# Gate units between the first dense units, one power for all key norms, keys a group ahead, and the last head's squares by one-column products

## The chip, the cores and the metric

The kernel runs on one core of a Trainium2 chip. The metric is the device time of one execution in microseconds (us). The core has five engines that the text calls PE (TensorE, the matmuls; PEld is its weight load), DVE (VectorE), ACT (ScalarE), POOL (GpSimd) and SP (SyncE, which here only issues transfers). Each engine takes its instructions in a fixed order, and they meet at semaphores.

## The reference

Two layers over a sequence of 512 tokens, 1024 channels, all in float32. Cut to what matters:

```python
h = rmsnorm(x, pre_mix_g)
proj = h @ w_in                  # q k v z beta decay | SWA q k v | gate A, gate B
y_a = deltanet_branch(...) @ w_up_dn      # 8 heads of 128
y_b = swa_sink_branch(...) @ w_up_sw      # 16 query heads of 64, 2 key heads, window 128
mix = (sigmoid(gate_a) * y_a + sigmoid(gate_b) * y_b) @ w_o
x = x + rmsnorm(mix, post_mix_g)
x = x + rmsnorm(square(relu(rmsnorm(x, pre_mlp_g) @ w_ff1)) @ w_ff2, post_mlp_g)
```

In the DeltaNet branch the keys are scaled to length one (`k * rsqrt(sum(k*k) + EPS)`), a triangular system per chunk and head is solved, a state runs over the chunks, and each head's output is normed: `rmsnorm(o, norm_g) * silu(z)`. The mean of squares of that norm is the "squares" of the title, one number per token and head.

## The kernel before

Activations lie channel by token, `128 x 512` tiles, eight of them for 1024 channels. Every float32 product is made of three passes: each operand is split in a high part (`_h`, rounded) and a low part (`_l`, the rest), and PE runs high by high, low by high and high by low. One **unit** (`mm_a`) makes 128 output channels for all 512 tokens: 8 blocks of 128 input channels x 3 passes = 24 matmuls of 512 columns. A split is one ACT copy (line 419 for weights, 545 for the rest) and one DVE subtraction (420, 546). Weights come in 512 KB chunks over SP, in the fixed order of `chunk_order`, four units ahead (`LOOK`).

A layer goes through these stages; the numbers are the spans in layer 0 of the profile shown below.

- Key, gate and attention stage (about 77 to 234 us). A loop over 16 attention groups `(t, g, e)`: four token tiles `t`, two key heads `g`, two halves `e`. `MIX` says which units ride with each group: `K` a key unit of the DeltaNet branch (`k_unit`), `G` a unit of gate B, `A` one of gate A. Three gate A units are made here (`NA = 3`).
  - `k_unit(h)` makes the keys of a head, their products with themselves in PSUM (`ps_a`, line 909, a ring of one bank called `PK`), takes the diagonal for the squared length (914), adds EPS (916), raises it to the power 0.5 on POOL (918, `irk`), and scales the products by the decay (926) into the triangular matrix `uu`.
  - `att_group` takes the scores (`ps_s`, 1055), a softmax with ACT and DVE, turns the probabilities (`ps_pt`, a bank of the `PS` ring of three), masks them on POOL (`pc`, 1095) and multiplies by the values (`ps_o`, 1102, also `PS`). `att_prep(t)` readies the keys `kT` and values of a token tile; it is called at the start of the tile's first group, after that group's unit in program order.
- First dense units, upward product and solve (about 223 to 299 us). `d_dense(0)` makes value, query and output gate units of head 0 (`ps_vp`, `ps_qp`, `ps_zp`), which use the `PM` ring of two banks; a bank of `vp` or `qp` is held until the causal convolution on DVE (883) has read it. Then eight units of the attention's upward product (`ps_us`) run, with the steps of the triangular solve on DVE between them, and then two gate A units (`NA` to `NA2`, `ps_ga`), stored to DRAM (`gad`).
- Heads (about 299 to 490 us). For each head, `d_inverse` finishes the inverse by small products (`ps_i`), `d_chain` runs the recurrence, and `d_dense(h + 1)` gives PE wide matmuls in between. `d_keys` loads the keys back (`kk`, ring `T[3]`) and `by_token` turns them through DRAM (1236, 1239, 1241). After head 7, three more gate A units run.
- The norm of each head is `d_tail(h)`, a generator whose steps are called by `d_step`: split the squares `w`, sum over channels with a product by ones (`ps_w`), copy one row out, store it to DRAM (`sd`), load it turned (`ff`, so that 512 numbers lie in 128 x 4), take the power -0.5 on POOL (1303), store (`fd`), broadcast to all partitions (`fb`, 1307), and multiply into `y1` (1309).
- Upward product of the DeltaNet branch (`ps_ud`, 490 to 535 us): `yT`, the split of each head's `y1` (line 546), then eight units, the first four of which take heads 0 to 5 before heads 6 and 7. Then output projection, and the MLP.

The order on each engine is not the program order. A planner lays it out ahead of time, from modelled durations: of what it reckons ready it issues, in the main, what stands earliest in the program. Buffers are rings of named tags (`T[0]` to `T[8]`, four each). `tc.keep_in_program_order(i)` keeps an instruction from being put ahead of earlier instructions of its engine.

Of the kernel before, what the change touches and what calls it, by code (L numbers as in the profile page):

```python
# [10 lines left out]
F32 = mybir.dt.float32  # L11
# [9 lines left out]
P = 128  # L21
# [39 lines left out]
def chunk_order(depth):  # L61


    out = []
    for l in range(depth):
        a_in = lambda w, c: out.append(("chunk", w, l, 0, c, 0))
        b_in = lambda w, r, c, n: out.append(("chunk", w, l, r, c, n))
        for a, b in BK:
            out.append(("chunk", "w_bkv", l, a * P, 0, (b - a) * NB))
        for u in range(NQU):  # L70
            a_in("w_q", u * 8)
        n_ = {"K": 0, "G": 0, "A": 0}
        for c in "".join(MIX):
            a_in("w_in", {"K": OFF_K, "G": OFF_GB, "A": OFF_GA}[c] + n_[c] * P)
            n_[c] += 1
        for h in range(H):
            for o in (OFF_V, OFF_Q, OFF_Z):
                a_in("w_in", o + h * P)
            if h == 0:
                for m in range(KT):  # L80
                    a_in("w_up_sw", m * P)
                for m in range(NA, NA2):
                    a_in("w_in", OFF_GA + m * P)
        for m in range(NA2, KT):
            a_in("w_in", OFF_GA + m * P)
        for m in range(KT):
            a_in("w_up_dn", m * P)
        for n in range(2):
            for j in range(4):
                b_in("w_o", j * 256, n * 512, 512)  # L90
        for s in range(4):
            out.append(("up", l, s))
            if s < 3:
                out.append(("seven", "w_ff2", l, s * 1024))
                continue
            for n in range(2):
                for j in range(4):
                    b_in("w_ff2", s * 1024 + j * 256, n * 512, 512)
    return out
# [44 lines left out]
def hybrid_trunk(ctx, tc, x, positions, pre_mix_g, dn_conv_w, dn_a_log, dn_dt_bias, dn_norm_g,  # L144
# [25 lines left out]
    def s1(name, n):  # L170
        return sm.tile([P, n], F32, name=name, bufs=1)
# [14 lines left out]
    def PK(name):  # L186
        return pp.tile([P, 512], F32, name=name, tag="pk", bufs=1)
# [27 lines left out]
    def c4(ap):  # L215
        return ap.rearrange("p (c i) -> p c i", c=4)
# [15 lines left out]
    nc.gpsimd.memset(ban, 0.0)  # L232
    nc.gpsimd.affine_select(out=ban, in_=ban, pattern=[[-1, P]], compare_op=ALU.is_ge, fill=NEG,
                            base=0, channel_multiplier=1)
    pw = const.tile([P, 8], F32, name="pw")
    nc.gpsimd.memset(pw[:, 0:4], -0.5)
    nc.gpsimd.memset(pw[:, 4:8], 0.5)
    mhalf, phalf = pw[:, 0:4], pw[:, 4:8]

    T64 = const.tile([64, 256], F32, name="T64")  # L240
    nc.gpsimd.memset(T64, 0.0)
# [298 lines left out]
    def split(src, hi, lo, sign=1.0):  # L540
        if sign < 0:
            act(out=hi, in_=src, func=AF.Copy, scale=-1.0)
            stt(out=lo, in0=src, scalar=-1.0, in1=hi.bitcast(F32), op0=ALU.mult, op1=ALU.subtract)
            return
        nc.scalar.copy(hi, src)
        tt(out=lo, in0=src, in1=hi.bitcast(F32), op=ALU.subtract)  # L546

    def pair(U, name):
        return U(name + "_h", F32R), U(name + "_l", F32R)
# [100 lines left out]
    for l in range(depth):  # L650
# [238 lines left out]


        cj, irk = [], []

        def k_unit(h):
            if h < 4:
                d = T[5]("D")
                dma(d, dd[h])
            else:
                d = decay_load(h)
            ps = PM("ps_kp")
            mm_a(ps, hT)  # L900
            k_ = conv_silu(ps, 8 + h, T[4], "kk")
            dma(kkd[h], k_)
            if h >= 4:
                decay_of(h, d)
            yield
            ps = PK("ps_a")
            for c in range(NC):
                sl = slice(c * P, (c + 1) * P)
                mm(ps[:, sl], lhsT=k_[:, sl], rhs=k_[:, sl], start=True, stop=True)
            u_ = T[5]("uu")  # L910
            sk_ = sm.tile([P, NC], F32, name="ssk")
            for c in range(NC):
                sl = slice(c * P, (c + 1) * P)
                stt(out=u_[:, sl], in0=ps[:, sl], scalar=1.0, in1=ident, op0=ALU.mult,
                    op1=ALU.mult, accum_out=sk_[:, c:c + 1])
            ts(out=sk_, in0=sk_, scalar1=EPS, scalar2=None, op0=ALU.add)
            ir = sm.tile([P, NC], F32, name="irk", bufs=H + 1)
            ptt(out=ir, in0=sk_, in1=phalf, op=ALU.pow)
            irk.append(ir)
            cc = sm.tile([P, NC], F32, name="cj", bufs=H + 1)  # L920
            nc.vector.reciprocal(cc, sk_)
            tt(out=cc, in0=cc, in1=hc(beta)[:, h, :], op=ALU.mult)
            cj.append(cc)
            for c in range(NC):
                sl = slice(c * P, (c + 1) * P)
                stt(out=u_[:, sl], in0=ps[:, sl], scalar=cc[:, c:c + 1], in1=d[:, sl],
                    op0=ALU.mult, op1=ALU.mult)
            dma(umat(h), c4(u_))
# [20 lines left out]
        def ga_early(m):  # L949
            ga_unit(m, T[5])  # L950
            dma(gad[m], sga[m])
# [82 lines left out]

        def att_group(t, g, e):

            if g == 0 and e == 0:
                if t == 0:
                    att_rope(0)
                att_prep(t)  # L1040
            if (g, e) == (1, 0) and t < NT - 1:
                att_rope(t + 1)
            w0 = max(t - 1, 0) * P
# [33 lines left out]
            for j in range(4):  # L1077
                js = slice(j * P, (j + 1) * P)
                act(out=M[:, js], in_=M[:, js], func=AF.Copy, scale=den[:, j:j + 1])
            yield  # L1080
            ps = PS("ps_pt")
            together = Order(nc.tensor)
# [34 lines left out]
        def steps(n):  # L1117
            for _ in range(n):
                next(sol, None)
# [30 lines left out]
        for u in klate:  # L1150
            fin(u)


        dn = {}

# [134 lines left out]
        def d_tail(h):  # L1290

            w, y1 = dn.pop(("t", h))
            wh, wl = pair(T[5], "w")
            split(w, wh, wl)
            ps = PS("ps_w")
            mm(ps, lhsT=ones_r, rhs=wh, start=True, stop=False)
            mm(ps, lhsT=ones_r, rhs=wl, start=False, stop=True)
            nc.scalar.copy(w[0:1], ps[0:1])
            dma(sd[h:h + 1, :], w[0:1])
            yield  # L1300
            ff = sm.tile([P, NC], F32, name="ff")
            dma(ff, sd[h, :].rearrange("(p j) -> p j", p=P))
            ptt(out=ff, in0=ff, in1=mhalf, op=ALU.pow)
            pdma(fd[h, :].rearrange("(p j) -> p j", p=P), ff)
            yield
            fb = T[6]("fb")
            dma(fb, fd[h, :].partition_broadcast(P))
            yield
            tc.keep_in_program_order(tt(out=y1, in0=y1, in1=fb, op=ALU.mult))

        tails = [d_tail(h) for h in range(H)]

# [64 lines left out]
        for t in range(NT):  # L1377
            tsl = slice(t * P, (t + 1) * P)
            for g in range(2):
                for j in range(g * 4, g * 4 + 4):  # L1380
                    hi, lo = oT[j]
                    split(qt[t][:, j * P:(j + 1) * P], hi[:, tsl], lo[:, tsl])
        turn0 = d_dense(0, lambda: steps(2))
        for m in range(KT):
            ps = PM("ps_us")
            mm_a(ps, oT)
# [3 lines left out]
            steps(2 if m < 6 else 40)  # L1390
            if m == 1:
                turn0()
        for m in range(NA, NA2):
            ga_early(m)

        Pcv, Tcv = inv

        d_load(0, 1, 2, 3)
# [385 lines left out]
```

## Time and profile before

| | |
|---|---|
| median of 3 runs | 1817.6 us (1817.01 to 1820.55) |
| the profiled execution's own time | 1817.76 us |
| its span, first to last instruction | 1816.1 us |
| busy: PE, DVE, ACT, POOL | 1787.7, 1376.8, 998.8, 200.3 us |
| mean granted TensorE clock | 0.998 |

Wide matmuls are pipelined: the profile shows each as 0.39 us long, and one starts every 0.227 us. So a PE that is shown busy can still lose time where two starts lie further apart, and such gaps are read from the starts.

### The profile page before, as it was taken

The numbers are of one execution on the slowest core, as the hardware profiler recorded it, in microseconds if no ns is written. First come the engines' busy times: TensorE is split into PE (matmuls) and PEld (weight loads), VectorE is DVE, ScalarE is ACT, GpSimd is POOL, SyncE is SP. The second block draws the span as 40 slices with busy tenths as digits, with TensorE's granted clock in tenths as the row PEclk, the third lists the DMA queues.
The fourth block names the chain that finished last, engine by engine and source line by source line (L and its number), as shares of the span: only waits on it lengthen the run. The fifth ranks groups of instructions, "written<-read, shape, count | busy, mean of one in ns | idle before, by whom it ended". The sixth has DMA issues, their size and how long they took to land.

```text
span 1816.1 us, 28412 instructions
## 1 busy us (share of the span) xinstructions
PE 1787.7 (98%) x10220; PEld 1511.2 (83%) x10220; DVE 1376.8 (76%) x2576; ACT 998.8 (55%) x2039; POOL 200.3 (11%) x346
## 2 busy tenths in 40 slices
PE   9999999999999999999999999999999999999998
PEld 7887878887788888989888877888877888889896
DVE  6489796888666878888565897878884669698973
ACT  7578732444434656566555887234443347566572
POOL 2013202221101000000020131022111010000000
PEclk9999999999999999999999999999999999999999
DMA  6845447555453255554557453575554533555551
GB/s 221 276 142 184 117 139 232 169 163 152 128 190 135 82 163 153 173 179 147 185 182 239 156 169 105 170 231 162 159 139 148 167 116 104 175 164 161 174 178 55
DMA packets 167071, 294.33 MB, mean 162 GB/s; under 512 B 34497, under 2 KB 83969, under 8 KB 166930
## 3 DMA queue, kind: packets, MB, share of 16 engines
q1 hardware_dynamic: 166418, 292.48, 51.9%
q8 instruction: 80, 1.31, 0.3%
q14 instruction: 61, 0.50, 0.1%
q0 software_dynamic: 512, 0.03, 0.0%
HBM read 246.19 MB, written 46.27 MB: 161 GB/s over the span
## 4 chain that ended last, share of the span: by engine, by line
PE 80%; DVE 8%; ACT 6%; DMA 3%; issue 2%; POOL 1%; SPq 0%; DVEq 0%; POOLq 0%; ACTq 0%
PE ps_f L435 2%; PE ps_f L436 2%; PE ps_f L437 2%; PE ps_zp L435 2%; PE ps_zp L436 2%; PE ps_b L506 2%; PE ps_us L436 2%; PE ps_b L504 2%; PE ps_b L508 2%; PE ps_us L437 2%; PE ps_us L435 2%; PE ps_zp L437 2%; PE ps_ud L436 1%; PE ps_qp L435 1%; PE ps_qp L436 1%
## 5 line engine op out<-in xcount | busy, mean ns | idle before, releaser
L419 ACT CAST wh<-wr 128x1024 fp32r<-128x1024 f32 (+2 forms) x366 | 372.7, 1023 | 416.1 <-PE ps_us L436 62.7
L420 DVE TENSOR_TENSOR wl<-wr,wh 128x1024 fp32r<-128x1024 f32 (+2 forms) x366 | 435.4, 1196 | 170.3 <-ACT wh L419 164.4
L571 POOL TENSOR_TENSOR pr<-pq,pw 128x1 f32<-128x1 f32 x16 | 9.8, 615 | 787.6 <-DVE pq L570 787.6
L435 PE MATMUL ps_f<-g_h,wh 128*128 128x512 f32 x160 | 62.4, 390 | 0.0
L436 PE MATMUL ps_f<-g_l,wh 128*128 128x512 f32 x160 | 62.4, 390 | 0.0
L437 PE MATMUL ps_f<-g_h,wl 128*128 128x512 f32 x160 | 62.2, 389 | 0.0
L1073 ACT ACTIVATE M<-M,nm 128x128 f32<-128x128 f32 x128 | 49.8, 390 | 10.9 <-DVE nm L1068 10.8
L436 PE MATMUL ps_ud<-yT_l,wh 128*128 128x512 f32 x128 | 50.7, 396 | 2.9 <-DVE yT_l L546 2.9
L435 PE MATMUL ps_zp<-h_h,wh 128*128 128x512 f32 x128 | 50.5, 394 | 2.8 <-DVE vv L883 2.8
L436 PE MATMUL ps_qp<-h_l,wh 128*128 128x512 f32 x128 | 53.2, 415 | 0.0
L437 PE MATMUL ps_qp<-h_h,wl 128*128 128x512 f32 x128 | 53.1, 415 | 0.0
L435 PE MATMUL ps_vp<-h_h,wh 128*128 128x512 f32 x128 | 52.8, 413 | 0.0
L437 PE MATMUL ps_vp<-h_h,wl 128*128 128x512 f32 x128 | 52.6, 411 | 0.0
L435 PE MATMUL ps_qp<-h_h,wh 128*128 128x512 f32 x128 | 52.5, 410 | 0.0
L435 PE MATMUL ps_ga<-h_h,wh 128*128 128x512 f32 x128 | 51.4, 402 | 1.0 <-ACT sga L946 1.0
L378 DVE TENSOR_TENSOR wr<-wr 128x512 f32<-128x512 f32 x72 | 47.5, 685 | 6.0 <-DMA wr<-in_weights_dram 5.5
L435 PE MATMUL ps_kp<-h_h,wh 128*128 128x512 f32 x128 | 51.5, 403 | 0.0
L436 PE MATMUL ps_vp<-h_l,wh 128*128 128x512 f32 x128 | 51.2, 400 | 0.0
L435 PE MATMUL ps_gb<-h_h,wh 128*128 128x512 f32 x128 | 51.2, 400 | 0.0
L437 PE MATMUL ps_ga<-h_h,wl 128*128 128x512 f32 x128 | 50.5, 395 | 0.0
L437 PE MATMUL ps_ud<-yT_h,wl 128*128 128x512 f32 x128 | 50.5, 395 | 0.0
L436 PE MATMUL ps_ga<-h_l,wh 128*128 128x512 f32 x128 | 50.5, 394 | 0.0
(449 smaller groups left out, 5958.3 us busy)
## 6 DMA issues: line engine op xcount, KB each, us to landing
wr<-in_weights_dram SPq DMA_DIRECT2D x336, 512.0 KB, 3.7
qT<-qd SPq DMA_DIRECT2D x32, 256.0 KB, 3.5
D<-dd SPq DMA_DIRECT2D x24, 256.0 KB, 2.8
xd<-xo SPq DMA_DIRECT2D x12, 512.0 KB, 2.6
xt<-xd SPq DMA_DIRECT2D x24, 256.0 KB, 6.1
qd<-qf_h SPq DMA_DIRECT2D x16, 256.0 KB, 4.2
qd<-qf_l SPq DMA_DIRECT2D x16, 256.0 KB, 3.4
D<-gd SPq DMA_DIRECT2D x16, 256.0 KB, 4.2
```

Source lines behind the costliest of these rows:

```text
L378: tt(out=o_, in0=i0, in1=i1, op=ALU.add)
L419: nc.scalar.copy(wh[:, :w], wr[:, :w])
L420: sub(out=wl[:, :w], in0=wr[:, :w], in1=wh[:, :w].bitcast(F32), op=ALU.subtract)
L435: mm(ps, lhsT=wh[:, k, :], rhs=hi, start=k == 0, stop=False)
L436: mm(ps, lhsT=wh[:, k, :], rhs=lo, start=False, stop=False)
L437: mm(ps, lhsT=wl[:, k, :], rhs=hi, start=False, stop=k == KT - 1)
L504: mm(pss[t], lhsT=hi[:, tsl], rhs=wh[:, r, :], start=k == 0 and not onto, stop=False, skip_group_check=onto)
L506: mm(pss[t], lhsT=hi[:, tsl], rhs=wl[:, r, :], start=False, stop=False, skip_group_check=onto)
L508: mm(pss[t], lhsT=lo[:, tsl], rhs=wh[:, r, :], start=False, stop=k == KT - 1, skip_group_check=onto)
L571: ptt(out=r, in0=q1, in1=mhalf[:, 0:1], op=ALU.pow)
L1073: act(out=M[:, j * P:(j + 1) * P], in_=M[:, j * P:(j + 1) * P], func=AF.Exp, bias=nm[:, j:j + 1], accum_out=den[:, j:j + 1])
```

## The change

- **Gate units.** The two gate A units `NA` to `NA2` no longer follow the eight `ps_us` units. One is made after the value unit of `d_dense(0)` and one after its query unit, through the call `after()`. Their weight chunks move in `chunk_order` to match.
- **One power.** `k_unit` writes the squared lengths of all heads in one tile `ssk` of 128 x 32. The eight powers of 128 x 4 on POOL become one of 128 x 32 after the attention loop.
- **Bank of the key products.** `ps_a` of odd heads takes a bank of `PS` instead of `PK`.
- **Keys ahead.** `att_prep(t + 1)` is called in the last group of tile `t`, after its softmax.
- **Last head.** For head 7 the squares are summed by four products with one column of ones, whose result already lies as 128 x 4. The split, the product by ones, the row's store and its load go. `fd` is then in another order, and the multiplication reads `fb` with a step of four elements. The multiplications of heads 6 and 7 are no longer kept in program order.

```diff
         for h in range(H):
             for o in (OFF_V, OFF_Q, OFF_Z):
                 a_in("w_in", o + h * P)
+                if h == 0 and o != OFF_Z:
+                    a_in("w_in", OFF_GA + (NA + (o == OFF_Q)) * P)
             if h == 0:
                 for m in range(KT):
                     a_in("w_up_sw", m * P)
-                for m in range(NA, NA2):
-                    a_in("w_in", OFF_GA + m * P)
...
+        ssk = s1("ssk", 32)
...
-            ps = PK("ps_a")
+            ps = (PS if h % 2 else PK)("ps_a")
...
-            sk_ = sm.tile([P, NC], F32, name="ssk")
+            sk_ = hc(ssk)[:, h, :]
...
-            ir = sm.tile([P, NC], F32, name="irk", bufs=H + 1)
-            ptt(out=ir, in0=sk_, in1=phalf, op=ALU.pow)
-            irk.append(ir)
...
-            if g == 0 and e == 0:
-                if t == 0:
-                    att_rope(0)
-                att_prep(t)
+            if (t, g, e) == (0, 0, 0):
+                att_rope(0)
+                att_prep(0)
...
+            if (g, e) == (1, 1) and t < NT - 1:
+                att_prep(t + 1)
             yield
...
+        ir = s1("irk", 32)
+        ptt(out=ir, in0=ssk, in1=pwide, op=ALU.pow)
+        irk = [hc(ir)[:, h, :] for h in range(H)]
...
             w, y1 = dn.pop(("t", h))
-            wh, wl = pair(T[5], "w")
-            split(w, wh, wl)
             ps = PS("ps_w")
-            mm(ps, lhsT=ones_r, rhs=wh, start=True, stop=False)
-            mm(ps, lhsT=ones_r, rhs=wl, start=False, stop=True)
-            nc.scalar.copy(w[0:1], ps[0:1])
-            dma(sd[h:h + 1, :], w[0:1])
-            yield
             ff = sm.tile([P, NC], F32, name="ff")
-            dma(ff, sd[h, :].rearrange("(p j) -> p j", p=P))
+            last = h == H - 1
+            if last:
+                for c in range(NC):
+                    mm(ps[:, c:c + 1], lhsT=w[:, c * P:(c + 1) * P], rhs=ones[:, 0:1], start=True,
+                       stop=True)
+                nc.scalar.copy(ff, ps[:, 0:NC])
+            else:
...
             ptt(out=ff, in0=ff, in1=mhalf, op=ALU.pow)
             pdma(fd[h, :].rearrange("(p j) -> p j", p=P), ff)
             yield
             fb = T[6]("fb")
             dma(fb, fd[h, :].partition_broadcast(P))
             yield
-            tc.keep_in_program_order(tt(out=y1, in0=y1, in1=fb, op=ALU.mult))
+            if last:
+                tt(out=c4(y1), in0=c4(y1), in1=fb.rearrange("p (q c) -> p c q", c=NC), op=ALU.mult)
+                return
+            m_ = tt(out=y1, in0=y1, in1=fb, op=ALU.mult)
+            if h < H - 2:
+                tc.keep_in_program_order(m_)
...
-        turn0 = d_dense(0, lambda: steps(2))
+        early_ga = list(range(NA, NA2))
+
+        def between():
+            steps(2)
+            if early_ga:
+                ga_early(early_ga.pop(0))
+
+        turn0 = d_dense(0, between)
...
-        for m in range(NA, NA2):
-            ga_early(m)
```

More of the change, by code (lines that the diff above doesn't have):

```diff
@@ L234, in hybrid_trunk @@
                             base=0, channel_multiplier=1)
-    pw = const.tile([P, 8], F32, name="pw")
+    pw = const.tile([P, 36], F32, name="pw")
     nc.gpsimd.memset(pw[:, 0:4], -0.5)
-    nc.gpsimd.memset(pw[:, 4:8], 0.5)
-    mhalf, phalf = pw[:, 0:4], pw[:, 4:8]
+    nc.gpsimd.memset(pw[:, 4:36], 0.5)
+    mhalf, pwide = pw[:, 0:4], pw[:, 4:36]
     T64 = const.tile([64, 256], F32, name="T64")
@@ L1292, in d_tail @@
             w, y1 = dn.pop(("t", h))
-            wh, wl = pair(T[5], "w")
-            split(w, wh, wl)
             ps = PS("ps_w")
-            mm(ps, lhsT=ones_r, rhs=wh, start=True, stop=False)
-            mm(ps, lhsT=ones_r, rhs=wl, start=False, stop=True)
-            nc.scalar.copy(w[0:1], ps[0:1])
-            dma(sd[h:h + 1, :], w[0:1])
-            yield
-            ff = sm.tile([P, NC], F32, name="ff")
-            dma(ff, sd[h, :].rearrange("(p j) -> p j", p=P))
+            ff = sm.tile([P, NC], F32, name="ff")
+            last = h == H - 1
[5 more added lines that the diff above has]
+            else:
+                wh, wl = pair(T[5], "w")
+                split(w, wh, wl)
+                mm(ps, lhsT=ones_r, rhs=wh, start=True, stop=False)
+                mm(ps, lhsT=ones_r, rhs=wl, start=False, stop=True)
+                nc.scalar.copy(w[0:1], ps[0:1])
+                dma(sd[h:h + 1, :], w[0:1])
+                yield
+                dma(ff, sd[h, :].rearrange("(p j) -> p j", p=P))
             ptt(out=ff, in0=ff, in1=mhalf, op=ALU.pow)
```

## The prediction

> **What bounds the kernel.** First the busy totals and the chain that ended last, then who waited for whom on PE.
>
> ```profile
> PE 1787.7 (98%) x10220; PEld 1511.2 (83%) x10220; DVE 1376.8 (76%) x2576; ACT 998.8 (55%) x2039; POOL 200.3 (11%) x346
> ...
> PE 80%; DVE 8%; ACT 6%; DMA 3%; issue 2%; POOL 1%; SPq 0%; DVEq 0%; POOLq 0%; ACTq 0%
> ```
>
> PE is the bound: 98% busy, 80% of the chain. The change takes practically no product away, so it can only win where PE stands still. The waits of PE, all that bear on the change (us in total, times, longest):
>
> ```profile
> PE ps_o L1102 <- POOL pc L1095: 3.6, 6, 0.8
> PE ps_ud L436 <- DVE yT_l L546: 2.9, 2, 2.1
> PE ps_zp L435 <- DVE vv L883: 2.8, 2, 1.4
> ...
> PE ps_a L909 <- DVE uu L926: 1.5, 4, 0.6
> PE ps_s L1055 <- ACT kT_h L1024: 1.0, 2, 0.5
> ```
>
> Each of the five parts of the change has its line here: gate units the `ps_zp` line, the power perhaps the `ps_o` line, the bank the `ps_a` line, the keys the `ps_s` line, the last head the `ps_ud` line. Together 11.8 us in two layers, 0.65% of the time; that is the size of the game. The profiled execution took 1817.76 us, 0.16 above the median of 1817.6; sums are made against 1817.8.
>
> **Gate units.** The wait they are put into, and the one they used to cover:
>
> ```profile
> 237.40 0.39 PE L437 MATMUL ps_qp<-h_h,wl 128*128 128x512 f32 x1
> 239.16 0.47 PE L435 MATMUL ps_zp<-h_h,wh 128*128 128x512 f32 x1 [1.38 <-DVE vv L883]
> 236.71 2.31 DVE L883 SCALAR_TENSOR_TENSOR vv<-ps_vp,cw,vv 128x509 f32<-128x509 f32 x3
> 286.58 1.80 SPq L1247 DMA_DIRECT2D kk<-kkd  x2
> 288.25 0.39 PE L435 MATMUL ps_ga<-h_h,wh 128*128 128x512 f32 x1
> 293.38 0.71 DVE L1236 STREAM_TRANSPOSE kvx<-kk 128x512 f32<-128x512 f32 x1 [2.79 <-DMA kk<-kkd]
> 299.22 0.21 PE L1191 MATMUL ps_i<-Tc,ur 32*32 32x32 f32 x1
> L1325 PE MATMUL ps_qk<-qq,kk x8: 275/275/377, 299.6 to 300.5; 128*128 128x128 f32 x8
> ```
>
> `ps_zp` starts 1.76 us after the last matmul of `ps_qp`, 1.5 more than the step of 0.227: with two `PM` banks it needs the value unit's bank, and DVE reads that until 239.0. With a gate unit in second place, the third unit meets the same late bank at about the same time; but the gate's own bank is free after one tanh of some 0.6 us, so I expect 0.7 of the 1.5 to stay and 0.8 to go, per layer (bounds 0 and 1.5). What a moved unit takes along: 24 matmuls, a weight load and a `gad` store on SP, one ACT cast, one DVE subtraction, one tanh; all are issued some 50 us sooner, on SP ahead of the `mbd` stores and the solve's transfers, and nothing there waits on them.
>
> The cover that goes: from 288.25 to 299.22 the two units ran while the keys came back. `kk` sits in ring `T[3]`, which the upward product's operand `oT` fills until its last unit, so the load at 286.58 goes out only then; it landed at 293.38, 5.1 us after that product ended, and was needed by `ps_qk` only at 299.6. After the change the product ends about 10 us later and `ps_qk` follows at once. PE has filler (`d_dense(1)`, 3 units of 24 x 0.227 = 16.3 us), but its order is fixed beforehand, and if the planner takes the load for shorter than it is, PE waits up to 5.1 - 0.4 = 4.7 us, or nothing if it does not. Four loads of `ur` ran ahead of `kk` before and will not now, so I take the low side: 0.8 per layer. The part's net: 0 (bounds +4.7 and -1.5 per layer).
>
> **Power and bank.**
>
> ```profile
> L918 POOL TENSOR_TENSOR irk<-ssk,pw x16: 1006/1008/1027, 102.1 to 1084.5; 128x4 f32<-128x4 f32 x16
> L571 POOL TENSOR_TENSOR pr<-pq,pw x16: 537/540/922, 563.8 to 1810.8; 128x1 f32<-128x1 f32 x16
> POOL pc L1095 <- ACT pf_h L545: 91.0, 16, 11.0
> 187.93 1.01 POOL L918 TENSOR_TENSOR irk<-ssk,pw 128x4 f32<-128x4 f32 x1 [1.65 <-DVE ssk L916]
> L909 PE MATMUL ps_a<-kk x128: 270/275/377, 97.1 to 1081.8; 128*128 128x128 f32 x128
> 104.92 0.28 PE L1056 MATMUL ps_s<-kT_l,qT 128*128 128x128 f32 x1
> 105.73 0.94 PE L909 MATMUL ps_a<-kk 128*128 128x128 f32 x6 [0.54 <-DVE uu L926]
> sum 80.00, PE 76.98 PEld 63.96 DVE 72.19 ACT 66.14 POOL 18.61; mean PE 19.24 PEld 15.99 DVE 18.05 ACT 16.54 POOL 4.65
> ```
>
> Eight powers of 1.01 us leave POOL per layer. One of 32 columns comes: from 0.54 for one column and 1.01 for four, 0.157 a column, 0.54 + 31 x 0.157 = 5.4 us at most, 1.0 at least. It can run when the last head's power ran, at 187.93, and is needed once head 0's chain has begun, at 299.6; POOL is busy 18.6 of 80 us in the stage (last row, 100 to 180 us), so I cost it at nothing. The cover is this slack; without it a `pc` behind it would come up to 5.4 us late. POOL's masks wait for ACT's casts (91.0 us, 16 times), which the power doesn't change, so I take no gain from the `ps_o` line.
>
> The bank: `ps_a` of head 1 waits for head 0's only bank, 0.7 us between starts at 105. With the four waits of the table (1.5 idle, some 0.2 more each in the starts) 2.3 us can go. But in this stage DVE is busy 72 of 80 us and it is DVE that frees banks, so half of it comes back as another wait: -1.2 in all. Below: 0; above: the key products hold a `PS` bank, 8.6 us for head 0 (97.1 to 105.7), for each of 8 odd heads, that `ps_pt` and `ps_o` also need (a rival below).
>
> **Keys ahead.**
>
> ```profile
> 153.21 0.39 PE L436 MATMUL ps_gb<-h_l,wh 128*128 128x512 f32 x1
> 154.12 0.50 PE L1055 MATMUL ps_s<-kT_h,qT 128*128 128x256 f32 x2 [0.52 <-ACT kT_h L1024]
> ```
>
> The scores of tile 2 lose 0.7 us here waiting for their keys (0.91 between starts). The same ACT casts and DVE subtractions now stand a group, some 9 us, earlier in priority. Per layer one such wait: 1.4 us can go. They delay other DVE work of the group by as much, so I take -1.0 (bounds 0 and -1.4).
>
> **Last head.** Layer 0's end of the branch, by engine in order of time:
>
> ```profile
> 485.77 1.77 POOL L1303 TENSOR_TENSOR ff<-ff,pw 128x4 f32<-128x4 f32 x1 [16.02 <-DMA ff<-sd]
> 487.83 0.62 POOL L1304 DMA_DIRECT2D fd<-ff  x1 [0.30 <-POOL ff L1303]
> 491.37 0.61 ACT L545 CAST yT_h<-yf 128x512 fp32r<-128x512 f32 x1
> 491.40 0.32 SPq L1307 DMA_DIRECT2D fb<-fd  x1
> 491.02 1.23 DVE L420 TENSOR_TENSOR wl<-wr,wh 128x1024 fp32r<-128x1024 f32 x1 [1.31 <-ACT wh L419]
> 496.08 0.69 DVE L1309 TENSOR_TENSOR yf<-yf,fb 128x512 f32<-128x512 f32 x1 [3.84 <-DMA fb<-fd]
> 496.69 0.68 DVE L546 TENSOR_TENSOR yT_l<-yf,yT_h 128x512 fp32r<-128x512 f32 x1
> 497.43 0.50 PE L436 MATMUL ps_ud<-yT_l,wh 128*128 128x512 f32 x1 [0.85 <-DVE yT_l L546]
> 501.45 0.32 SPq L1307 DMA_DIRECT2D fb<-fd  x1
> 505.81 0.69 DVE L1309 TENSOR_TENSOR yf<-yf,fb 128x512 f32<-128x512 f32 x1 [8.43 <-DMA fb<-fd]
> ```
>
> The multiplication at 496.08 is head 6's, at 505.81 head 7's. PE waits for a `yT_l` of an earlier head, whose cast was done at 491.98: it stands in DVE's queue behind head 6's multiplication, which waits for its broadcast. So the last head isn't what PE waits for; the queue behind head 6 is. The change shortens head 7's chain (two transfers gone), takes the split (one ACT, one DVE instruction) out ahead of that cast, and gives back the ring places of `w` and `fb` sooner; and head 6's multiplication need no longer keep its place. The planner can then put the `yT_l` first, at about 492.3, and the wait goes. In layer 1 it is longer and has a sequel:
>
> ```profile
> 1395.25 0.69 PE L436 MATMUL ps_ud<-yT_l,wh 128*128 128x512 f32 x1 [2.07 <-DVE yT_l L546]
> 1396.17 0.63 PE L435 MATMUL ps_ud<-yT_h,wh 128*128 128x512 f32 x1
> 1395.00:1399.00 4.00, 3.75 (x10) 2.93 (x10) 0.20 (x1) 0.24 (x1) 1.07 (x2) 0.57 0.73 277
> ```
>
> After it the granted clock was 0.57 over 4 us, 4 x 0.43 = 1.7 us lost. The waits are 0.85 + 2.07 idle and 0.2 more each in the starts, 3.3; with the clock 5.0. I take -5.0, all of it (bounds: that, and +6.8, below).
>
> The Trainium skill (TensorE: Matmul & The Clock Gate, Part 1: The HAM clock gate) lets the clock fall to half after an idle window of about 3.4 us. By that a wait of 2.07 us would not have cost it and the term would be 3.3; the trace shows 0.57, and goes before.
>
> Head 7's own pieces: two `ps_w` matmuls of 512 columns (0.45) go; four one-column products come, bounded by 0 and by `ps_qk`'s eight instructions in 0.9 us. Even, 0.
>
> **Sum.** 0 - 1.2 - 1.0 - 5.0 = -7.2: 1817.8 - 7.2 = 1810.6, against the median 1810.4.
>
> **The rivals.**
> - **Keys uncovered.** PE waits for `kk` at `ps_qk` by 2.5 us a layer instead of 0.8: +3.4, 1814.0. For it: 5.1 us between product's end and landing; against: 16.3 us of filler.
> - **The tail wait stays.** Head 6's chain itself is untouched, and if the planner has its broadcast landed by 492, the multiplication still goes first: the -5.0 is gone, 1815.6.
> - **The last head goes first (slower).** In `d_step(H-1, H-2, H-3)` head 7's power and store now precede head 6's. If POOL and SP take them in that order, head 6's store leaves one power and one issue (1.77 + 0.62 + 0.3 = 2.7 us) later; if `yT_l` is still behind its multiplication, each layer loses 2.7 more, and the clock falls in layer 0 too (1.7, less what overlaps, 1.4): 1817.8 - 2.2 + 5.4 + 1.4 = 1822.4. It decides once `yT_l` ends after some 499. Against: head 6's `ff` is there at 485.7, before head 7's sums can be.
> - **`PS` too small.** Eight odd heads cost 0.8 each in `ps_pt` or `ps_o`: +6.4, 1817.0: nothing is gained.
>
> **How the numbers follow.** Forecast 0.48 (its own range 1806 to 1814), keys 0.14, tail stays 0.15, last head first 0.13, `PS` 0.10. About 0.2%, 3.6 us, is what a measurement tells from no change. Faster than 1814.0 takes the forecast and half of the keys: 0.55. Slower than 1821.2: the third rival and part of the fourth, 0.16. Same: 0.29. The range reaches from 1806 (forecast with all of the bounds) to 1820, leaving out the third rival and a little below.
>
> **What would show it.** The `ps_ud` line gone from PE's waits and no granted clock under 1 at the end of layer 1's branch; `yT_l` ahead of head 6's multiplication; `ps_zp`'s wait replaced by a shorter one at `ps_qp`; no wait at `ps_qk` for `kk`; the `ps_a` and `ps_s` lines gone without new `ps_pt` or `ps_o` lines. A wait at `ps_ud` of 3 us or more in both layers would make it wrong.

## The result: slower by 0.84%, and the profile after

The changed kernel took 1833.57 us (median of 6 runs, 1831.55 to 1834.53) against 1817.91 for the kernel before on the same chip: a ratio of 1.0084, 95% interval 1.0070 to 1.0098. The ratio goes by the means of the fast runs alone, which leaves out one run of the kernel before, of 5820.85 us, and so it is not quite the quotient of the two medians. The forecast was 1810.4.

The profile page of the changed kernel, busy totals and the chain that ended last:

```profile
PE 1794.0 (98%) x10232; PEld 1516.6 (83%) x10232; DVE 1372.0 (75%) x2574; ACT 998.2 (55%) x2037; POOL 196.1 (11%) x332
...
PE 83%; DVE 7%; ACT 4%; DMA 2%; issue 2%; POOL 1%; SPq 0%; DVEq 0%; POOLq 0%; ACTq 0%
```

PE does the same work (12 matmul records more, from the one-column products), yet its busy time is 6.3 us longer and the span (1829.9 us) 13.8 us longer. So PE stood still more, and more of its work ran on a slow clock: apart from the last few us of each profile, the granted clock stands at 0.50 for one stretch of 3.41 us in the kernel before (from 1395.39) and for five in the changed kernel (from 178.24, 499.09, where two follow each other, 1055.46 and 1407.04). PE was busy for 3.4 us of the one and 15.4 us of the five; half of the difference, some 6 us, is an estimate of what the clock costs. The waits of PE in the changed kernel (us in total, times, longest):

```profile
PE ps_ud L436 <- DVE yT_l L546: 7.5, 2, 3.9
PE ps_a L910 <- DVE kk L887: 5.6, 4, 2.1
PE ps_qp L435 <- DVE vv L883: 2.8, 2, 1.4
...
PE ps_s L1053 <- DVE kT_l L1023: 2.1, 2, 1.1
...
PE ps_pt L1084 <- DVE uu L924: 1.4, 2, 0.7
```

The `ps_ud` wait that should have gone is 2.6 times as long, and there is a wait that the profile of the kernel before does not show: `ps_a` for the convolved keys `kk`. To see what that makes, the layer is cut at the first matmul of `ps_gb`, `ps_vp`, `ps_i`, `ps_ud` and `ps_wo` (their starts are read from the timeline). Times in us, layer 0 and layer 1:

| stretch | before | after | difference, both layers |
|---|---|---|---|
| attention stage (`ps_gb` to `ps_vp`) | 150.2, 150.2 | 153.8, 154.2 | +7.5 |
| first dense units, upward product, gate units (`ps_vp` to `ps_i`) | 76.1, 76.0 | 76.1, 76.0 | 0.0 |
| heads (`ps_i` to `ps_ud`) | 190.7, 190.8 | 191.2, 190.2 | -0.1 |
| tail (`ps_ud` to `ps_wo`) | 66.5, 69.3 | 71.8, 71.3 | +7.2 |

Two stages carry it all. **The tail** of layer 0, engines mixed in one timeline (start, duration, engine, line; in brackets the idle time before and what ended it):

```profile
488.66 1.38 POOL L1313 TENSOR_TENSOR ff<-ff,pw 128x4 f32<-128x4 f32 x1 [15.31 <-ACT ff L1303]
490.99 1.03 POOL L1313 TENSOR_TENSOR ff<-ff,pw 128x4 f32<-128x4 f32 x1
...
494.77 0.61 ACT L545 CAST yT_h<-yf 128x512 fp32r<-128x512 f32 x1
497.83 1.07 DVE L1320 TENSOR_TENSOR yf<-yf,fb 128x512 f32<-128x512 f32 x1 [8.69 <-DMA fb<-fd]
498.81 1.22 DVE L420 TENSOR_TENSOR wl<-wr,wh 128x1024 fp32r<-128x1024 f32 x1
499.95 1.29 DVE L546 TENSOR_TENSOR yT_l<-yf,yT_h 128x512 fp32r<-128x512 f32 x2
500.69 0.80 PE L436 MATMUL ps_ud<-yT_l,wh 128*128 128x512 f32 x1 [3.60 <-DVE yT_l L546]
501.15 0.69 DVE L1322 TENSOR_TENSOR yf<-yf,fb 128x512 f32<-128x512 f32 x1
```

Head 7's power (it waited for the copy at line 1303) runs ahead of head 6's, and head 7's multiplication (line 1320) ahead of head 6's (1322). Head 5's `yT_h` is cast by 495.4; its `yT_l` stands in DVE's queue behind head 7's multiplication, which waits for its broadcast until 497.83, and behind a weight difference. PE waits for it. And the window behind (length, then busy us and count of PE, PEld, DVE, ACT, POOL, then granted clock, DMA share, GB/s):

```profile
501.00:506.00 5.00, 5.00 (x13) 3.86 (x13) 1.53 (x3) 0.62 (x1) 0.00 (x0) 0.51 1.06 397
```

After the wait, 13 matmuls lie in 5 us where 22 would at a step of 0.227 us: the granted clock was 0.51.

**The attention stage**, again one timeline of several engines:

```profile
164.64 0.63 POOL L821 TENSOR_SCALAR_AFFINE_SELECT D<-D 128x512 f32<-128x512 f32 x1 [4.16 <-DMA D<-gd]
165.30 0.21 ACT L823 ACTIVATE egl<-D 128x4 f32<-128x4 f32 x1 [1.66 <-POOL D L821]
167.16 0.63 POOL L821 TENSOR_SCALAR_AFFINE_SELECT D<-D 128x512 f32<-128x512 f32 x1 [1.31 <-DMA D<-gd]
167.83 0.21 ACT L823 ACTIVATE egl<-D 128x4 f32<-128x4 f32 x1 [1.01 <-POOL D L821]
...
169.26 1.03 ACT L419 CAST wh<-wr 128x1024 fp32r<-128x1024 f32 x1
170.32 1.23 DVE L420 TENSOR_TENSOR wl<-wr,wh 128x1024 fp32r<-128x1024 f32 x1 [4.01 <-ACT wh L419]
171.84 0.67 ACT L880 ACTIVATE kk<-ps_kp,cw 128x512 f32<-128x512 f32 x1
176.93 1.16 PE L910 MATMUL ps_a<-kk 128*128 128x128 f32 x8 [2.06 <-DVE kk L887]
```

ACT waits twice for a decay matrix (`D`, loaded from DRAM, masked on POOL); the weight cast, a softmax and the start of the keys' convolution stand behind it. DVE, the busiest engine after PE here, is idle 4.01 us, then late, and PE waits 2.06 us. The same place in the kernel before:

```profile
165.59 0.39 ACT L1073 ACTIVATE M<-M,nm 128x128 f32<-128x128 f32 x1
...
168.03 0.21 ACT L823 ACTIVATE egl<-D 128x4 f32<-128x4 f32 x1 [1.87 <-POOL D L821]
168.15 1.03 ACT L419 CAST wh<-wr 128x1024 fp32r<-128x1024 f32 x1
169.08 0.68 ACT L880 ACTIVATE kk<-ps_kp,cw 128x512 f32<-128x512 f32 x1
```

There ACT waits for `D` too, but the softmax (line 1073) is done before that wait and the scaling of `D` (825) comes only after the weight cast and the start of the convolution, which begins 2.8 us sooner than in the changed kernel. So the wait is not new; what stands behind it is. The window of 80 us that the prediction showed for the kernel before, now in the changed kernel, and the one behind the wait:

```profile
100.00:180.00 80.00, 74.47 (x392) 61.97 (x391) 69.03 (x212) 64.57 (x200) 11.67 (x14) 0.99 0.51 162
176.00:182.00 6.00, 5.07 (x26) 4.58 (x27) 5.97 (x23) 4.83 (x16) 0.80 (x2) 0.72 0.26 87
```

PE was busy 76.98 of these 80 us before and is 74.47 now; DVE 72.19 and 69.03. POOL went from 18.61 to 11.67: the powers have left, and POOL is not what is short.

### The profile page after: what moved, and what is told of

Its sections match the earlier page's. It is cut to its first block, busy times and chain, and to the rows that moved or that the text cites. A ratio compares the mean times of both kernels' runs of the same rounds, so it can differ in the third digit from the quotient of the medians.

```text
span 1829.9 us, 28406 instructions
## 1 busy us (share of the span) xinstructions
PE 1794.0 (98%) x10232; PEld 1516.6 (83%) x10232; DVE 1372.0 (75%) x2574; ACT 998.2 (55%) x2037; POOL 196.1 (11%) x332
## 4 chain that ended last, share of the span: by engine, by line
PE 83%; DVE 7%; ACT 4%; DMA 2%; issue 2%; POOL 1%; SPq 0%; DVEq 0%; POOLq 0%; ACTq 0%
PE ps_f L435 2%; PE ps_f L436 2%; PE ps_f L437 2%; PE ps_qp L435 2%; PE ps_qp L436 2%; PE ps_ud L436 2%; PE ps_qp L437 2%; PE ps_b L504 2%; PE ps_us L437 2%; PE ps_b L506 2%; PE ps_b L508 2%; PE ps_us L436 2%; PE ps_us L435 2%; PE ps_ud L437 2%; PE ps_zp L435 1%
## 5 line engine op out<-in xcount | busy, mean ns | idle before, releaser
L435 PE MATMUL ps_ud<-yT_h,wh 128*128 128x512 f32 x128 | 51.1, 402 | 0.0
```

The source lines that it names most:

```text
L435: mm(ps, lhsT=wh[:, k, :], rhs=hi, start=k == 0, stop=False)
```

## The experiments

Line numbers in an experiment's rows are its own. The ratios are to the kernel before, in runs on the same chip, with 95% intervals. The stages are those of the table above, both layers summed, from one profiled execution each:

| kernel | attention | tail | ratio |
|---|---|---|---|
| before | 300.4 | 135.9 | 1 |
| the changed kernel | 307.9 | 143.1 | 1.0084 (1.0070 to 1.0098) |
| e1 old tail | 308.7 | 132.5 | 1.0042 (1.0029 to 1.0054) |
| e5 pinned | 305.5 | 142.1 | 1.0085 (1.0068 to 1.0101) |
| e6 steps 5, 6, 7 | 307.4 | 130.8 | 1.0020 (1.0010 to 1.0029) |
| e7 two heads, steps 5, 6, 7 | 305.4 | 130.6 | 1.0023 (1.0015 to 1.0032) |
| e2 one pool | 308.2 | 140.2 | 1.0095 (1.0081 to 1.0109) |
| e3 keys at their tile | 299.6 | 142.5 | 1.0054 (1.0042 to 1.0067) |
| e4 own powers | 307.1 | 142.1 | 1.0087 (1.0074 to 1.0101) |
| e8 before + keys ahead | 307.4 | 135.5 | 1.0044 (1.0030 to 1.0057) |
| e10 decays later | 296.2 | 143.2 | 1.0034 (1.0022 to 1.0046) |
| e11 = e3 + e6 | 299.1 | 130.9 | 0.9978 (0.9970 to 0.9987) |
| e12 before + last head, steps 5, 6, 7 | 299.7 | 130.9 | 0.9978 (0.9969 to 0.9987) |
| e13 = e6 + e10 | 296.4 | 130.9 | 0.9965 (0.9951 to 0.9978) |
| e14 = e13 without keys ahead | 297.3 | 130.9 | 0.9972 (0.9962 to 0.9982) |
| e15 = e13 with one pool | 297.1 | 130.8 | 0.9977 (0.9965 to 0.9988) |
| e16 before + steps 5, 6, 7 | 301.8 | 133.8 | 1.0002 (0.9993 to 1.0011) |
| e17 before + decays later | 298.0 | 132.4 | 0.9988 (0.9979 to 0.9997) |

How far one profile can be trusted is in the table too: the changed kernel, e1, e5, e6 and e7 have the same attention code and show 305.4 to 308.7; before, e8 and e17 have the same tail code and show 135.9, 135.5 and 132.4.

### The tail

**e1, the old tail.** `d_tail` as before, nothing else undone.

```diff
+            wh, wl = pair(T[5], "w")
+            split(w, wh, wl)
...
-            last = h == H - 1
-            if last:
...
+            tc.keep_in_program_order(tt(out=y1, in0=y1, in1=fb, op=ALU.mult))
```

> The changed kernel with the tail of the last head as it was before (squares by rows of ones, four steps, every multiplication pinned); the other three parts stay. Theory T (the last head goes first): the tail stage lost 5.26 us in layer 0 and 1.97 us in layer 1 to head 7's power, store and load standing ahead of head 6's and to the clock that drops in the wait that follows; with the old tail these 7.2 us come back, 1826.4 us, and the wait at ps_ud falls from 3.8 and 4.1 us to about 2. Rival: the tail is late because everything before it is placed otherwise (the attention stage left other work behind); then the time stays at 1832 or more.

Measured: tail 132.5 instead of 143.1, ratio 1.0042.

```profile
PE ps_ud L436 <- DVE yT_l L546: 1.1, 2, 0.6
```

The part of the last head costs 0.42% as it is written, half of the loss. What remains lies in the attention stage. This does not yet tell which piece of the part it is.

**e5, the multiplications of heads 6 and 7 kept in order.**

```diff
-                tt(out=c4(y1), in0=c4(y1), in1=fb.rearrange("p (q c) -> p c q", c=NC), op=ALU.mult)
+                tc.keep_in_program_order(tt(out=c4(y1), in0=c4(y1), in1=fb.rearrange("p (q c) -> p c q", c=NC), op=ALU.mult))
...
-            if h < H - 2:
-                tc.keep_in_program_order(m_)
+            tc.keep_in_program_order(m_)
```

> The changed kernel with the multiplications of heads 6 and 7 kept in the written order again; the last head still by one-column products, its steps still first. Theory T1 (GpSimd's and SyncE's order: head 7's power, store and load go first, so head 6's load lands 3 to 5 us later than before): the pins change nothing, since VectorE met both loads late; ratio to before 1.007 to 1.010, ps_ud still waits 3.5 to 4.5 us. Theory T2 (the loosened order on VectorE, which put head 7's multiplication ahead of head 6's): with the pins the tail gets back 3 us or more a stage, ratio 1.005 or less.

```profile
PE ps_ud L436 <- DVE yT_l L546: 7.4, 2, 4.0
```

Unchanged, 1.0085. The loosened pins are not the cause: in the written order head 7's multiplication comes first anyway.

**e6, the steps of the last heads in the order 5, 6, 7.** One line.

```diff
-            d_step(H - 1, H - 2, H - 3)
+            d_step(H - 3, H - 2, H - 1)
```

> The changed kernel with the steps of the last heads in the order 5, 6, 7 (d_step(H - 3, H - 2, H - 1)), so that head 6's power, store and load stand ahead of head 7's. Theory T1: head 6's power waits for its row of sums (4 us on the way), head 7's behind it; head 6's multiplication comes back to some 7 us after head 6's sums, head 7's a little behind: the wait at ps_ud falls from 4 to 1.5 to 2.5 us, the tail is 3 to 7 us shorter over both layers, ratio 1.0045 to 1.007. Rival: with the order turned, GpSimd waits for the row of head 6 with head 7's power behind it, so that the wait only changes its head: ps_ud waits 3.5 us or more all told, ratio 1.007 to 1.010.

Measured: tail 130.8, shorter than in the kernel before; ratio 1.0020. The size was better than theory T1 had it, and its reason was wrong. The timeline, and a window:

```profile
490.10 1.39 POOL L1313 TENSOR_TENSOR ff<-ff,pw 128x4 f32<-128x4 f32 x1 [15.11 <-ACT ff L1303]
496.20 0.61 ACT L545 CAST yT_h<-yf 128x512 fp32r<-128x512 f32 x1
496.99 0.69 DVE L546 TENSOR_TENSOR yT_l<-yf,yT_h 128x512 fp32r<-128x512 f32 x1
501.76 0.69 DVE L1322 TENSOR_TENSOR yf<-yf,fb 128x512 f32<-128x512 f32 x1 [4.09 <-DMA fb<-fd]
502.97 1.07 DVE L1320 TENSOR_TENSOR yf<-yf,fb 128x512 f32<-128x512 f32 x1 [0.51 <-DMA fb<-fd]
```

```profile
498.00:502.00 4.00, 4.00 (x20) 3.28 (x19) 0.24 (x1) 0.00 (x0) 0.00 (x0) 1.00 0.79 190
```

GpSimd still takes head 7's power first, and both multiplications come even later than in the changed kernel (501.76 and 502.97, there 501.15 and 497.83). PE does not wait all the same, because head 5's `yT_l` is now ahead of both. So neither the late loads nor the one-column products cost the time: one DVE subtraction in the wrong place did.

**e7, one-column products for head 6 too.**

```diff
-            last = h == H - 1
+            last = h >= H - 2
...
-            d_step(H - 1, H - 2, H - 3)
+            d_step(H - 3, H - 2, H - 1)
```

> The changed kernel with the one-column products for head 6 too, the steps in the order 5, 6, 7, and head 6's multiplication kept in order. No row of sums goes through memory for either head. Theory T1 (what was wrong is head 6 behind head 7, not the products): head 6's power can start at 486, its load lands before ps_ud's first pass ends (496.7), head 7's as now at 497.8, and head 6's products (24 a layer, 5 us) cover that: ps_ud waits under 1 us, the tail is 4 to 6 us a layer shorter than the changed kernel's in layer 0 and 2 to 4 in layer 1, ratio 1.003 to 1.005, less than with the old tail (1.0042 was measured with it). Rival: the loads take as long as before when two are issued close together, and ps_ud waits 2 us or more as it did: ratio 1.006 or more.

Head 6's multiplication now starts at 491.66, ten us sooner than in e6, and head 7's at 498.60. The tail is 130.6 us, the ratio 1.0023: nothing more is gained. Once the split is in front, the time of the loads does not matter. (1.003 to 1.005 was expected: the theory behind it still took the loads for the cause.)

**e12 and e16, on the kernel before.** e12 takes over the part of the last head (`d_tail` of the change) with the steps in the order 5, 6, 7; e16 takes that order alone, which is its whole edit:

```diff
-            d_step(H - 1, H - 2, H - 3)
+            d_step(H - 3, H - 2, H - 1)
```

> The kernel before with the last head's part alone, but its steps in the order 5, 6, 7. Theory (what PE waits for is the split of head 5 behind a multiplication in VectorE's queue; here it goes first): both waits at ps_ud (0.85 and 2.07 us, 1.0 and 2.2 between starts) and the slow clock behind the second go, 5.0 us as the prediction had it: ratio 0.9965 to 0.998. Rival: with one-column products and the loosened multiplications PE waits for head 6 or 7 instead, later in ps_ud: 0.999 or more.

> The kernel before with nothing but the steps of the last heads in the order 5, 6, 7 (one line); rows of ones, four steps and all pins as before. If this order is all that the tail needed, the waits at ps_ud go: 0.9975 to 0.9985. If the split of head 5 only gets ahead because head 6's multiplication is no longer kept in order, or because the last head's chain takes other work from VectorE, ps_ud waits 0.85 and 2.07 us as before: 0.9995 to 1.0005.

e12: 0.9978, and PE has no wait for `yT_l` at `ps_ud`. The tail is 5.0 us shorter than in the profile before, as the prediction's term said; by the whole time the gain is 4.0 us (2.4 to 5.6), and with the same tail code as before e17 shows one wait of 0.6 us, no slow clock and only 132.4 us. So the 5.0 is the gain over one profile, at the upper end of what the tail before shows. e16: 1.0002, PE still waits (1.00 and 1.09 us). The order alone is not enough, since there head 6's multiplication (at 498.29) still runs ahead of the split (498.90); part and order are needed together. Which piece of the part it takes, the loosened multiplications or the shorter chain, was not separated.

### The attention stage

The expectations weigh three theories: P, that the order on ACT (decays ahead of other work) is the cause, in e4 with the single power as the reason for that order; C, the bank of the key products; D, the keys ahead.

**e2, one pool.**

```diff
-            ps = (PS if h % 2 else PK)("ps_a")
+            ps = PK("ps_a")
```

> The changed kernel with all key products in one PSUM pool again (the line ps = PK for every head). Theory C (the bank): the odd heads' products hold a bank of PS, so ps_pt and ps_o wait (0.84 and 1.00 us in layer 0, 0.9 in layer 1, seen as starts of ps_pt, ps_o and ps_su that come late); the attention stage gets back 1.5 to 2 us a layer, 1830 us. Theory P (the late convolution, put there by the order of decays and casts on ScalarE): the bank has no part in it, and its own small gain of 1.2 us is lost again: 1833.6 to 1834.8 us, the attention stage as long as in the changed kernel.

1.0095, attention 308.2: no gain. Theory C fell; the bank is not what costs the time.

**e4, own powers.** Eight powers of 128 x 4 in the stage instead of one of 128 x 32.

```diff
...
+            ir = sm.tile([P, NC], F32, name="irk", bufs=H + 1)
+            ptt(out=ir, in0=sk_, in1=phalf, op=ALU.pow)
+            irk.append(ir)
...
-        ir = s1("irk", 32)
-        ptt(out=ir, in0=ssk, in1=pwide, op=ALU.pow)
-        irk = [hc(ir)[:, h, :] for h in range(H)]
```

> The changed kernel with a power for each head again (eight of 128x4 in the attention stage, none of 128x32 behind it). Theory P (the powers held the decays back): with the eight powers on GpSimd the planner again puts the decays of heads 6 and 7 behind the softmax on ScalarE, the convolution of the keys is in time, and the waits at ps_a (0.9 and 2.2 us a layer, with the half clock behind the second) go: the attention stage is 3 to 3.9 us a layer shorter, 1826 to 1827.5 us. Theories C and D: the powers have no part in it, 1832 to 1835 us, ps_a still waits for kk.

```profile
PE ps_a L909 <- DVE kk L887: 4.8, 3, 2.1
```

1.0087, and `ps_a` waits on. The single power has no part in the loss, though its own size was at the upper end (the last section).

**e3, keys at their tile; e8, keys ahead alone on the kernel before.** The two calls of `att_prep`, undone in the one, done alone in the other. The edit of e3; e8's is its reverse on the kernel before:

```diff
-            if (t, g, e) == (0, 0, 0):
-                att_rope(0)
-                att_prep(0)
+            if g == 0 and e == 0:
+                if t == 0:
+                    att_rope(0)
+                att_prep(t)
...
-            if (g, e) == (1, 1) and t < NT - 1:
-                att_prep(t + 1)
```

> The changed kernel with the keys of a tile prepared at that tile's first group, as before. Theory D (keys ahead): the planner, given the keys' transpose and copies behind the softmax of the group before, puts the copies and differences where they are late (ps_s waits 1.1 and 1.0 us for kT_l) and moves the softmax of other groups; taken back, the attention stage gets back the 2.1 us of that wait and some of the 0.9 and 2.2 us waits at ps_a too: 1826 to 1831 us. Theory P: only the ps_s wait changes its name, ps_a still waits for kk 2 us a layer: 1832 to 1834.6 us.

> The kernel before with one part of the change alone, the keys of a tile prepared in the last group of the tile before. Theory D (keys ahead moves ScalarE's order, whatever else is there): ps_a waits for kk and ps_s for kT_l, the attention stage is 2.5 to 4 us a layer longer, ratio 1.003 to 1.0045. Rival: it does that only together with the other parts (the bank, the single power), ratio 1.001 or less.

PE's waits in e3, then in e8:

```profile
PE ps_s L1053 <- ACT kT_h L1022: 2.3, 4, 0.6
...
PE ps_a L910 <- DVE kk L887: 1.0, 1, 1.0
```

```profile
PE ps_a L909 <- DVE kk L887: 5.4, 4, 2.1
...
PE ps_s L1055 <- DVE kT_l L1025: 2.1, 2, 1.1
```

Taken out of the changed kernel, the stage is 299.6 us, a little under that of the kernel before (300.4); put alone into the kernel before, it is 307.4 and the ratio 1.0044. The keys ahead are the whole loss of this stage, with or without the rest.

**e10, decays behind their own convolution, keys still ahead.**

```diff
+            order = Order(nc.scalar)
+            order.begin()
             k_ = conv_silu(ps, 8 + h, T[4], "kk")
             dma(kkd[h], k_)
             if h >= 4:
                 decay_of(h, d)
+            order.end()
```

> The changed kernel, keys ahead and all, with one order more: on ScalarE a head's decays (lines 823 and 825) stand behind that head's own convolution. Theory P (in the changed kernel the decays of heads 6 and 7, which wait 4 us for their load, stand on ScalarE ahead of the weight cast, the softmax and the convolution that PE needs next): ps_a no longer waits for kk (5.6 us in all), the attention stage is 2 to 4 us a layer shorter though the keys are still prepared ahead, ratio to before 1.004 to 1.006. Rival D (the copies of the keys ahead themselves take ScalarE and VectorE time from the group, whatever the decays do): ps_a still waits, or ps_s and ps_pt wait as long in its place, ratio 1.0075 or more.

```profile
164.45 0.69 ACT L880 ACTIVATE kk<-ps_kp,cw 128x512 f32<-128x512 f32 x1 [0.34 <-PE ps_kp L437]
167.95 1.05 ACT L419 CAST wh<-wr 128x1024 fp32r<-128x1024 f32 x1
168.90 0.63 ACT L886 ACTIVATE th<-kk 128x512 f32<-128x512 f32 x1
169.43 0.20 ACT L823 ACTIVATE egl<-D 128x4 f32<-128x4 f32 x1
...
172.04 1.05 PE L913 MATMUL ps_a<-kk 128*128 128x128 f32 x8
```

```profile
100.00:180.00 80.00, 78.17 (x420) 66.14 (x419) 73.55 (x230) 68.21 (x211) 13.45 (x15) 1.00 0.52 165
```

Weight cast and convolution first, the decay behind them without a wait on POOL; the wait of `ps_a` for `kk` is down from 5.6 us to 0.2 in all, and the stage takes 296.2 us, 11.7 less than in the changed kernel and 4.2 less than before. Ratio 1.0034, below what theory P expected. So in this stage the keys ahead do harm only through the place that the planner then gives the decays. Why it gives them that place was not traced; e10 fixes the place without touching the keys.

**e17, the same order on the kernel before.** The edit is e10's.

> The kernel before with nothing but the order on ScalarE, decays behind their own convolution. If the decays cost something in the kernel before too (its attention stage is 150.2 us, 148 with the order in the changed kernel): 0.9975 to 0.999. If they only get in the way with the keys ahead, 1.000 within 0.0007.

0.9988 (0.9979 to 0.9997): the order is worth about 2 us (0.5 to 3.8) there too, so not all of e10's stage is the change's merit.

### What is left when both orders are right

**e11 (e3 with e6), e13 (the change whole, with both orders), e14 (e13 without keys ahead), e15 (e13 with one pool).** Their edits are those shown above, put together.

> The changed kernel with the keys of a tile at that tile and the steps of the last heads in the order 5, 6, 7; gate units, one power, the bank and the one-column products stay. If the two causes add (keys ahead 0.30% by its own run, the steps' order 0.64%), the ratio to before is 1.0084 - 0.0030 - 0.0064 = 0.999, within 0.9975 to 1.000. If the attention stage's loss comes from somewhere else too, it stays above 1.001.

> The changed kernel whole, with both orders added: decays behind their own convolution on ScalarE, and the last heads' steps in the order 5, 6, 7. By theory P and the order of the tail both: 1.002 (measured with the tail's order alone) less 0.002 to 0.004, ratio 0.998 to 1.000. If the keys ahead cost time by themselves: 1.001 or more.

> The changed kernel with both orders added (decays behind their own convolution, last heads 5, 6, 7), but the keys of a tile at that tile. If keys ahead give what the prediction took for them (1.0 us, bounds 0 and 1.4) once ScalarE's order no longer turns against them: ratio to before 0.9965 + 0.0006 = 0.997, ps_s waits for kT_h again (1.0 us or more in all). If all of the 5 us between the two orders and the one without the decays' order is the decays' doing: 0.9965 or less.

> The changed kernel with both orders added, and all key products in one PSUM pool (PK) again. If the bank gives what the prediction took (1.2 us, bounds 0 and 2.3): ratio 0.997 to 0.998, ps_a waits for uu again. If the bank of PS that the odd heads hold costs as much in ps_pt and ps_o (ps_pt waits 1.3 us for uu): 0.9965 or less.

e11 was expected at 0.999 if the two causes add, and came out at 0.9978: undoing both brings back the whole loss, and a little more than their sum, by no more than the widths of the intervals added up allow. e13 is faster than both kernels: 1809.48 us against 1815.45, 0.9965 (0.9951 to 0.9978). Some of PE's waits in it:

```profile
PE ps_o L1104 <- POOL pc L1097: 2.8, 5, 1.0
...
PE ps_pt L1087 <- DVE uu L927: 1.3, 2, 0.7
...
PE ps_qk L1343 <- DMA kk<-kkd: 0.4, 1, 0.4
```

The `ps_ud`, `ps_a` and `ps_s` waits are gone or under 0.3 us. Undoing the keys (e14) or the bank (e15) lengthens the attention stage by 0.9 and 0.7 us, but that is inside the scatter of the profiles, and the ratios' intervals overlap. Whether those two parts are worth their microsecond stays open. For the bank the waits speak against it: with it `ps_pt` waits 1.3 us for `uu`, and without it (e15) that wait is gone and `ps_a` waits 1.3 us for `uu` in its place.

Where e13's gain comes from can be read off by adding: the last head's part with its steps in order (e12) gives 0.22%, the decays' order alone (e17) 0.12%, together 0.9966, and e13 measures 0.9965. The second of these is no part of the change. For gate units, power, bank and keys together nothing is left, within some 0.2%.

## Why the prediction was wrong

- **Gate units, net 0.** The number is right, 76.1 us both times, but by luck in part, since neither of its terms came out. The wait moved from `ps_zp` to `ps_qp` and is as long (2.8 us), so of the 0.8 us a layer that was to go nothing went. Nor were 0.8 us a layer lost on `kk`: in the changed kernel's profile PE has no wait at `ps_qk` for it. The cover is thinner all the same. Seven of the twelve experiments with moved gate units (e2, e4, e5, e6, e10, e13, e15) show one such wait, in layer 1, of 0.2 to 1.2 us; none of the five kernels with the gate units in their old place does.
- **Power, 0.** Right (e4).
- **Bank, -1.2.** Not contradicted: e2 and e15 are slower than their partners by 0.1%, with overlapping intervals. But the wait that was to go, `ps_a` for `uu` (1.5 us), came back almost whole as `ps_pt` for `uu` (1.4 us), where the prediction took half. The rival "`PS` too small" showed as a `ps_pt` wait of 1.4 us in all, not 6.4.
- **Keys ahead, -1.0, bounds 0 and -1.4.** This step failed first: the attention stage cost +7.5. The term was read from the wait that goes (1.4 us), and the bounds allowed no loss, though the text itself put the copies a group, some 9 us, earlier in priority. It named no instruction that they overtake or let through. What the planner then put ahead of the softmax and the convolution is ACT's decays, which wait for a DMA (e8, e10).
- **Last head, -5.0.** This failed second: +7.2. The mechanism was right (a split behind a multiplication in DVE's queue), and so, roughly, was the size of what could be won (e12: 5.0 us of stage in one profile, 4.0 us of the time). The step that failed is "the planner can then put the `yT_l` first": with head 7's steps called first, head 7's multiplication went ahead of it, and PE waited 3.60 us in layer 0 and 3.93 in layer 1, more than the 3 us that the prediction itself named as the sign of being wrong.
- **The rival "last head goes first"** had that loss, +6.8 us for the two layers against 7.2 measured, and its point of decision (the `yT_l` ends after 499; it ended at 500.6). That the sizes agree is partly luck: it blamed head 6's late store, with the split behind head 6's multiplication, while the split ran ahead of head 6's multiplication and behind head 7's. e6 shows the lateness to be harmless and the place on DVE to be all. Its chance of 0.13 was too low: the kernel's own text, `d_step(H-1, H-2, H-3)`, spoke for it.
- **The sum.** -7.2 was forecast. With both orders mended the same change gives 0.35% (0.22 to 0.49, read from the ratio's interval), 4.0 to 8.9 us of 1815.45. That this is near 7.2 is luck too, since about 2 us of it is the decays' order (e17) and the rest is the last head's; the 2.2 us for bank and keys were not seen. Both losses are orders on an engine's queue.

## What to carry to other kernels

Before crediting a shorter chain or an earlier start, list what each in-order engine would have to pass over: an instruction that waits for a DMA costs whatever stands behind it, even if its own result is not needed for a long time. A part that moves work earlier has a loss as its second bound, namely the wait of the overtaking instruction. And when a change loses time, compare the order on the engines before the durations: here two small edits of order turned 0.84% slower into 0.35% faster with no part taken out, though one of them, the decays' order, gives 0.12% without the change too.

## What the runs showed of the hardware

**The clock falls for 3.41 us at a time, and the length of a wait does not decide whether it does.** Wherever the clock fell in these eighteen profiles, apart from the last few us of each, it stood at 0.50 for 3.41 us or for two such stretches in a row. At full work that costs 1.7 us a stretch, half of the 3.41. In layer 1 of the changed kernel PE waited 0.73 and then 1.05 us, 1.6 us apart, and the next stretch has a clock of 0.50:

```profile
1052.86 1.16 PE L910 MATMUL ps_a<-kk 128*128 128x128 f32 x8 [0.73 <-DVE kk L887]
1055.48 0.58 PE L1053 MATMUL ps_s<-kT_l,qT 128*128 128x256 f32 x1 [1.05 <-DVE kT_l L1023]
```

```profile
1052.05:1055.46 3.41, 1.62 (x10) 1.15 (x9) 3.29 (x6) 3.36 (x15) 1.56 (x1) 1.00 0.20 77
1055.46:1058.87 3.41, 3.39 (x12) 2.89 (x13) 3.24 (x11) 2.76 (x10) 0.00 (x0) 0.50 0.50 177
1058.87:1062.28 3.41, 3.41 (x18) 2.88 (x17) 2.50 (x11) 3.03 (x6) 0.64 (x1) 1.00 0.42 133
```

In e2 (layer 0) a longer wait, of 2.89 us, left the clock at 1.00:

```profile
501.42 0.50 PE L436 MATMUL ps_ud<-yT_l,wh 128*128 128x512 f32 x1 [2.89 <-DVE yT_l L546]
```

```profile
503.00:506.41 3.41, 3.41 (x17) 2.83 (x16) 0.69 (x1) 0.23 (x1) 0.00 (x0) 1.00 1.05 395
```

The same wait can go either way: 2.06 us for `kk` cost a slow stretch in the changed kernel (0.72 over the six us from 176) and none in e5, where it ends at 176.28. So the 1.7 us that the prediction added for the clock, rightly read from its profile, is no fixed part of that wait, and it is one reason why stages of the same code differ between profiles. What decides it was not settled: PE was busy 1.62 of the 3.41 us ahead of the fall above, and in e2 1.58 of the 3.41 us ahead of 503.00, where no fall came.

The Trainium skill (TensorE: Matmul & The Clock Gate, Part 1: The HAM clock gate) gives an idle window of about 3.4 us as what throttles the clock. Here the falls have that length, but one came behind waits of 0.73 and 1.05 us with a burst of work between them, and one behind a wait of 2.06 us, so the measurements differ from a rule that asks for a whole idle window.

**A power of 128 x 32 on GpSimd took 5.45 us**, the upper end of the estimate from one and four columns (5.4). The next mask `pc` ran only behind it, at 197.20; no PE wait for it is seen up to 206.

```profile
191.78 5.45 POOL L1154 TENSOR_TENSOR irk<-ssk,pw 128x32 f32<-128x32 f32 x1 [2.01 <-DVE ssk L917]
```
